# Attention scores of two heads side by side on 64 rows each, with queries and keys transposed before they are split

## The chip, the cores and the metric

The kernel runs on one core of a Trainium2 chip. The metric is the device time of one execution in microseconds (us); less is better. Engines: PE is TensorE (matmuls), PEld its weight loads, DVE VectorE, ACT ScalarE, POOL GpSimd, SP SyncE, which here only issues DMAs.

## The reference, cut to what matters

One inference step of a two-layer backbone with 640 tokens: 512 latent tokens, which are computed together with 128 prompt tokens. In every layer one input projection feeds three token mixers of head size 64; their outputs are gated, summed, projected, and followed by a squared-ReLU feed-forward. All is fp32.

```python
# A: differential attention, 4 pairs of heads, keys of 512 latent + 128 cached tokens
o1 = blocked_attention(q[:, :, :HA, None], k[:, :, :HA], v)[:, :, :, 0]
o2 = blocked_attention(q[:, :, HA:, None], k[:, :, HA:], v)[:, :, :, 0]
o = o1 - lam.astype(o1.dtype) * o2
# B: grouped-query attention, 8 heads of queries, 2 of keys, the same 640 keys
s = jnp.einsum('bqhgd,bkhd->bhgqk', qblk, k, preferred_element_type=jnp.float32) * scale
p = jax.nn.softmax(s, axis=-1).astype(v.dtype)
# C: neighbourhood attention, 8 heads: 256 keys around a tile of 128 queries, with a bias, and the 128 cached ones
p = jax.nn.softmax(jnp.concatenate([s_lat, s_ctx], axis=-1), axis=-1).astype(v.dtype)
```

The prompt's tokens attend to the 128 prompt keys alone.

## The kernel before, in words

**Precision.** The matmuls run on fp32r operands. Each fp32 operand is split in two parts: hi, a copy to fp32r (ACT), and lo, the rest (DVE, `value - hi`). A product with weights takes three matmuls: hi·hi, hi·lo, lo·hi. Transposes run on PE as well, through `tp` (line 246); every matmul goes through `mm` (line 243). As helpers record every operation, all ACT work stands under line 260, DVE's mostly under 265, with 278 for `stt`, and POOL's under 303 and 309.

**Issue order.** `Plan` (from line 56) records all instructions in program order and then writes down, with estimated durations, the order in which each engine issues them: each takes the first recorded of the instructions whose operands are there by the estimate (`schedule`, line 165). PSUM is followed bank by bank, in recorded order. `pl.bias` shifts an instruction's place in that order: the evacuation of a projection is moved forward (`EVAC`), the projection of mixers B and C back (`FILL`).

**Stages.** A layer has a mixer stage (`Phase1`) and then gates, branch and output projections and the feed-forward, which are products of 128 features by 640 tokens in pieces of 256 and 384 columns. The mixers go in 10 units of 384 columns of the input projection: 4 of A (two heads and one value of 128 each), 2 of B (four query heads, one key head), 4 of C (two heads). So the two layers have 8, 4 and 8 units. For each unit and each of 5 tiles of 128 tokens (order 0, 1, 4, 2, 3; tile 4 is the prompt), `project` (line 798) makes 24 matmuls of 384 columns into bank 0 or 1, and `evacuate` (line 806) takes the result apart: values, the norm in B, the rotary embedding in A and B, and then, from line 864, queries and keys. These are split into hi and lo while tokens still lie on partitions (two ACT and two DVE instructions), one of the two operands doubled, so that 128 columns hold hi and lo (or hi twice) of one head. Six fp32r transposes through bank 2 (`tz`) turn them, an ACT copy takes 512 columns out (scaled by 1/8) and a DVE copy 256.

**Scores.** Contraction rows 0 to 63 hold hi of a head's keys and rows 64 to 127 lo (for A and C), the queries are hi on both halves or lo on both. So two matmuls of 128 rows per head make all four products (`scores`, line 901; in B the roles are exchanged). `dense_row` (line 928) makes one head's scores of 128 queries by 640 keys in two banks of three (3, 4, 5), then the maximum (DVE), the exponential with its sum (ACT), and the row is scaled (POOL, in A the difference of the two heads). C takes 384 keys in one of the three banks.

**Values.** Probabilities are transposed in fp32, four blocks of 128 columns to a bank of `tb_` (banks 6 and 7), split while they leave PSUM (`split_T`, line 911), and multiplied with the values. In B and C a stationary tile holds hi and lo of the values, so the result's row halves are added (`fold`, line 1041). Outputs go to DRAM (`ospill`) and are read back by the next stage.

**Jobs.** A unit is 1 (A), 5 (B: four heads and the prompt) or 3 (C: two heads and the prompt) jobs of three stages: scores; transposes and values; A's norm. `step` (line 1185) records stage 3 of job i − 2, stage 1 of job i and stage 2 of job i − 1; the projections of the next unit are recorded after it.

## Time and profile before

| | |
|---|---|
| median of 3 runs | 2447.91 us (2447.16 to 2448.43) |
| span of the profiled execution, first to last instruction | 2446.9 us |
| another time of that execution | none is given; its span is the time that the rows are held against |
| instructions | 41996 |

The span is what the trace covers; the median is 1.0 us longer. A busy share counts the time in which at least one instruction of an engine is under way. Matmuls overlap in the array, so that the mean duration of one is longer than the distance from one to the next.

### The profile page before, as it was taken

To read this page: it belongs to the slowest core of one execution; us is meant where nothing else is said; L and a number is where in the kernel's file an instruction comes from. 1 tells how busy PE (TensorE), PEld (TensorE's weight loads), DVE (VectorE), ACT (ScalarE), POOL (GpSimd) and SP (SyncE) were. 2 spreads that over 40 slices of the span, in tenths; PEclk is the share of its full clock that TensorE was granted. 3 is DMA by queue.
4 is the path that set the end of the run, shared out by engine and by line. 5 is a ranking of instruction groups with operands and counts; after the bars stand their busy time and mean duration, and the time that the engine had idled before them with its cause. 6 is when DMAs were issued, how large, how long until landed. Compare 5 with 4: busy or idle time off the path is not lost. (4 is left out here: it accounts for less than half of the span.)

```text
span 2446.9 us, 41996 instructions
## 1 busy us (share of the span) xinstructions
PE 2376.5 (97%) x15796; PEld 2306.2 (94%) x15796; DVE 1601.8 (65%) x3615; ACT 1100.8 (45%) x2650; POOL 446.0 (18%) x527
## 2 busy tenths in 40 slices
PE   7898999999999999999999999999999999999998
PEld 5798999999999999999989988999999999999997
DVE  6878878789989994444477787765343674444445
ACT  4556677632333523222266567765223263223321
POOL 3536534200000000000034454321000000000000
PEclk8999999999999999999999999999999999999999
DMA  6211112466554552222231112225232222222221
GB/s 239 87 49 59 51 48 83 148 234 212 192 177 131 162 192 78 72 78 72 78 123 56 50 50 68 69 81 172 78 94 77 73 72 72 78 75 75 78 72 57
DMA packets 94960, 245.39 MB, mean 100 GB/s; under 512 B 11682, under 2 KB 23458, under 8 KB 93732
## 3 DMA queue, kind: packets, MB, share of 16 engines
q1 hardware_dynamic: 94756, 242.70, 30.5%
q8 instruction: 124, 2.03, 0.3%
q14 instruction: 80, 0.66, 0.1%
HBM read 225.62 MB, written 17.04 MB: 99 GB/s over the span
## 5 line engine op out<-in xcount | busy, mean ns | idle before, releaser
L243 PE MATMUL psm<-mr 128*128 128x384 f32 (+1 forms) x10656 | 1764.8, 319 | 17.6 <-ACT mr L260 8.6
L243 PEld LDWEIGHTS psm<-mr 128*128 128x128 f32 x10656 | 1631.2, 189 | 26.7 <-ACT mr L260 11.6
L260 ACT ACTIVATE mr<-mf 128x384 fp32r<-128x384 f32 (+2 forms) x928 | 445.3, 498 | 906.1 <-PE psm L243 868.4
L265 DVE TENSOR_TENSOR mr<-mf,mr 128x384 fp32r<-128x384 f32 (+3 forms) x796 | 419.3, 537 | 497.7 <-ACT mr L260 492.3
L309 POOL TENSOR_TENSOR mr<-mf,mr 128x384 fp32r<-128x384 f32 (+1 forms) x168 | 189.4, 1147 | 491.3 <-ACT mr L260 490.6
L243 PE MATMUL psm<-U,mr 128*128 128x256 f32 (+1 forms) x1788 | 277.6, 306 | 0.6 <-ACT mr L260 0.5
L243 PEld LDWEIGHTS psm<-U,mr 128*128 128x128 f32 x1788 | 264.4, 189 | 1.3 <-ACT mr L260 0.6
L309 POOL TENSOR_TENSOR mf<-mf 128x256 f32<-128x256 f32 (+3 forms) x93 | 89.9, 967 | 842.8 <-DVE mf L265 822.1
L303 POOL TENSOR_SCALAR mf<-mf 128x640 f32<-128x640 f32 (+3 forms) x236 | 144.3, 615 | 353.0 <-DVE mf L265 286.6
L292 DVE CUSTOM_DVE_ANT_0 psm<-mf,U1B 128x1024 f32<-128x1024 f32 x160 | 197.5, 1234 | 11.3 <-DMA mf<-wmod 9.9
L278 DVE SCALAR_TENSOR_TENSOR mf<-psm,mf 128x256 f32<-128x256 f32 (+2 forms) x484 | 171.3, 400 | 50.6 <-PE psm L243 42.2
L260 ACT ACTIVATE mf<-psm,mf 128x640 f32<-128x640 f32 (+3 forms) x256 | 162.5, 643 | 65.8 <-DVE mf L265 48.4
L260 ACT ACTIVATE mf<-mf 128x256 f32<-128x256 f32 (+5 forms) x305 | 140.4, 500 | 76.8 <-DVE mf L278 52.7
L265 DVE TENSOR_REDUCE mf<-psm 128x1 f32<-128x640 f32 (+2 forms) x212 | 148.2, 703 | 39.4 <-PE psm L243 33.8
L265 DVE TENSOR_TENSOR mr<-psm,mr 128x512 fp32r<-128x512 f32 (+2 forms) x252 | 140.9, 578 | 24.3 <-ACT mr L260 21.8
L260 ACT ACTIVATE mf<-psm 128x384 f32<-128x384 f32 (+7 forms) x266 | 104.1, 417 | 106.5 <-PE psm L243 102.5
L260 ACT ACTIVATE mr<-psm 128x512 fp32r<-128x512 f32 (+2 forms) x252 | 123.5, 513 | 53.2 <-PE psm L246 45.5
L246 PE MATMUL psm<-mf 128*128 128x128 f32 x752 | 119.6, 275 | 5.7 <-DVE mr L265 3.7
L265 DVE TENSOR_TENSOR mf<-psm,mf 128x128 f32<-128x128 f32 (+5 forms) x248 | 92.7, 390 | 46.2 <-ACT mf L260 24.3
L246 PEld LDWEIGHTS psm<-mf 128*128 128x128 f32 x752 | 89.8, 141 | 16.8 <-DVE mr L265 6.8
L246 PEld LDWEIGHTS psm<-mr 128*128 128x128 f32 x600 | 73.1, 141 | 33.5 <-DVE mr L265 20.1
L246 PE MATMUL psm<-mr 128*128 128x128 f32 x600 | 89.4, 242 | 12.4 <-DVE mr L265 9.5
(85 smaller groups left out, 1516.4 us busy)
## 6 DMA issues: line engine op xcount, KB each, us to landing
mf<-w SPq DMA_DIRECT2D x368, 384.0 KB, 3.0
mf<-wmod SPq DMA_DIRECT2D x84, 512.0 KB, 3.6
mf<-bias SPq DMA_DIRECT2D x8, 1024.0 KB, 5.2
U<-wmod SPq DMA_DIRECT2D x12, 512.0 KB, 5.9
mf<-x SPq DMA_DIRECT2D x16, 320.0 KB, 6.8
ospill<-mf SPq DMA_DIRECT2D x16, 256.0 KB, 2.4
newz<-mf SPq DMA_DIRECT2D x20, 192.0 KB, 1.9
U1A<-ospill SPq DMA_DIRECT2D x12, 320.0 KB, 2.9
```

Source lines behind the costliest of these rows:

```text
L243: self.add("PE", d, lambda R: self.nc.tensor.matmul(R(out), R(lhsT), R(rhs), start=start, stop=stop), [out], [lhsT, rhs])
L246: self.add("PE", 55 if in_.dtype == F32R else 108, lambda R: self.nc.tensor.transpose(R(out), R(in_), ident), [out], [in_, ident])
L260: self.add("ACT", d, lambda R: self.nc.scalar.activation(R(out), R(in_), func, **kw), outs, ins)
L265: self.add("DVE", d, lambda R: getattr(self.nc.vector, name)(R(out), *map(R, ins), *args, **kw), [out] + list(extra), list(ins) + [x for x ...
L278: self.add("DVE", d, lambda R: self.nc.vector.scalar_tensor_tensor(R(out), R(a), s, R(b), op0, op1), [out], [a, b] + ([s] if hasattr(s, "a ...
L292: self.add("DVE", d, lambda R: self.nc.vector.tensor_tensor_reduce(out=R(out), in0=R(a), in1=R(b), scale=1.0, scalar=0.0, op0=ALU.mult, op ...
L303: self.add("POOL", d, lambda R: self.nc.gpsimd.tensor_scalar(R(out), R(a), s1, s2, op0, op1), [out], [a] + [s for s in (s1, s2) if hasattr ...
L309: self.add("POOL", d, lambda R: self.nc.gpsimd.tensor_tensor(R(out), R(a), R(b), op), [out], [a, b])
```

## The change

- Queries and keys are no longer split before the transposes. Their fp32 values (in B after norm and rotary embedding, with the one key head copied beside itself by POOL; in C copied out of PSUM by ACT) are collected for tiles 0 and 1, for 4, and for 2 and 3 (`batch`), and then transposed in fp32, two heads of 64 features to a block: one block of queries (two in B) and one of keys per token tile. The transposes go through banks 6 and 7, and the split into hi and lo happens while the blocks leave PSUM.
- A head m has rows 64 m to 64 m + 63 of queries and keys. Its scores are three matmuls of 64 rows: hi·hi, hi·lo, lo·hi (lo·lo is dropped), recorded in turns for the two heads. Head 0 writes banks 2 and 4, head 1 banks 3 and 5 (`SC`); the prompt's scores go there too. `Plan.mm` counts half the time for a matmul of 64 rows.
- B's and C's jobs are now two heads by half of the latent tokens instead of one head by all. In C the value products of 4 × 512 columns per unit become 16 of 128 columns; those of 256 columns stay 16. Outputs of B and C are stored in halves of 256 tokens.
- Cached keys are no longer doubled in DRAM. The first unit's banks and the temporary places are rearranged, the feed-forward has 9 spare places instead of 10, comments are gone.

```diff
@@ Plan.mm
         if rhs.dtype == F32R:
             d = max(n, 256) / 2.4
+            if lhsT.ap[0][1] == 64:
+                d /= 2
@@ hybrid_plan
-    zb, tz, sb1, tb_ = Banks((0, 1)), psm[:, 2], Banks((3, 4, 5)), Banks((6, 7))
...
-            return (psm[:, 3:5], psm[:, 3:6:2], psm[:, 4:6])[(self.i - 1) % 3]
+    zb, tb_ = Banks((0, 1)), Banks((6, 7))
+
+    SC = [psm[:, 2 + m:6:2] for m in range(2)]
+    ROWSOF = (slice(0, 64), slice(64, 128))
+    PARTS = ((0, 0), (0, 1), (1, 0))
@@ Phase1
-            self.hl = r.ring(768, 2)
...
-            self.ck, self.cv = b.tile(256), b.tile(128)
+            self.ck, self.cv = b.tile(128), b.tile(128)
...
-            self.tmp = b.ring(320, 5)
+            self.src = b.ring(UW, 3)
+            self.tmp = b.ring(320, 4)
@@ Unit.cached
-            act(dst, ck, AF.Copy)
-            tt(dst[64:128], ck[64:128], f32(dst[64:128]), ALU.subtract)
+            self.split(self.kk[:, 0, k0:k0 + P], self.kk[:, 1, k0:k0 + P], ck)
@@ Unit.evacuate
+            elif self.k == "C":
+                src = p.src.get(nqk)
+                act(src, z[:, :nqk], AF.Copy)
...
-            self.split(t1[:, :, 0], t1[:, :, 1], s4[:, one])
-            self.split(t2[:, :, 0], t2[:, :, 1], s4[:, two].unsqueeze(2).to_broadcast([P, n2, 2, 64]))
-
-            tb = tz
-            for i in range(4):
-                tp(f32r(tb[:, i * P:(i + 1) * P]), hlt[:, i * P:(i + 1) * P], identr)
-            act(self.qall[:, :, c], tb.rearrange("p (f t) -> p f t", f=4), AF.Copy, scale=0.125)
-            for i in range(2):
-                tp(f32r(tb[:, i * P:(i + 1) * P]), hlt[:, (4 + i) * P:(5 + i) * P], identr)
...
+            ks = src[:, P:2 * P]
+            if self.k == "B":
+
+                ks = (p.src.get() if prompt else whole)[:, 2 * P:]
+                for h in range(prompt ^ 1, 2):
+                    pl.pts(ks[:, h * 64:(h + 1) * 64], src[:, 256:320], 1.0, 0.0, ALU.mult, ALU.add)
+            self.batch.append((t, src, ks))
+            if t in (1, 3, 4):
+                self.transposed()
+            pl.bias = 0
+
+        def transposed(self):
+
+            n, t0, nf = len(self.batch), self.batch[0][0], self.nf
+            m = n * P
+            c = slice(t0 * P, t0 * P + m)
+            qb = tb_.get()
+            kb, k0 = (tb_.get(), 0) if self.k == "B" else (qb, m)
+            for j, (_, src, ks) in enumerate(self.batch):
+                for f in range(nf):
+                    tp(qb[:, f * m + j * P:f * m + (j + 1) * P], src[:, f * P:(f + 1) * P], identf)
+                tp(kb[:, k0 + j * P:k0 + (j + 1) * P], ks, identf)
+            self.batch = []
+            qs = qb[:, :nf * m].rearrange("p (f t) -> p f t", f=nf)
+            act(self.q[:, :, 0, c], qs, AF.Copy, scale=0.125)
+            stt(self.q[:, :, 1, c], qs, 0.125, f32(self.q[:, :, 0, c]), ALU.mult, ALU.subtract)
...
+            for dst, d0, s0, s1 in pieces:
+                d = slice(d0, d0 + s1 - s0)
+                self.split(dst[:, 0, d], dst[:, 1, d], kb[:, k0 + s0:k0 + s1])
+
+
+        def scores(self, outs, f, c, keys):
+
+            for i, (x, y) in enumerate(PARTS):
+                for m in range(2):
+                    mm(outs[m], self.q[ROWSOF[m], f, x, c], keys(ROWSOF[m], y), i == 0, i == 2)
@@
-        def dense_row(self, h, c, sums):
...
+        def dense_rows(self, f, c, sums):
+
             for hf in range(2):
-                self.scores(sb[:, hf, :320], h, c, slice(hf * 320, (hf + 1) * 320))
-            nm = small.get()[:, :1]
-            pl.red(nm, sb[:, :, :320], AX.XY, ALU.max, negate=True)
+                kc = slice(hf * 320, (hf + 1) * 320)
+                self.scores([SC[m][:, hf, :320] for m in range(2)], f, c, lambda r, y: self.kk[r, y, kc])
+            rows = []
+            for m in range(2):
+                nm = small.get()[:, :1]
+                pl.red(nm, SC[m][:, :, :320], AX.XY, ALU.max, negate=True)
+                b, pt = self.p.pp.get()
+                act(pt.rearrange("p (f k) -> p f k", f=2), SC[m][:, :, :320], AF.Exp, bias=nm, accum=sums[m])
+                rows.append((b, pt))
+            return rows
@@ jobs
-                return [self.job_B(0, o), self.job_B_prompt()] + [self.job_B(m, o) for m in (1, 2, 3)]
-            o = {}
-            return [self.job_C(0, o), self.job_C_prompt(), self.job_C(1, o)]
+                return [self.job_B(0, 0), self.job_B_prompt(), self.job_B(0, 1), self.job_B(1, 0), self.job_B(1, 1)]
+            return [self.job_C(0), self.job_C_prompt(), self.job_C(1)]
@@ job_B
+            for qt in (2 * half, 2 * half + 1):
+                s = [small.get()[:, :1] for _ in range(2)]
+                r = self.dense_rows(f, slice(qt * P, (qt + 1) * P), s)
@@ job_C
+            for i, qt in enumerate((2 * half, 2 * half + 1)):
+                s3 = [SC[m][:, i, :384].rearrange("p (b k) -> p b k", b=3) for m in range(2)]
+                self.scores(s3, 0, slice(qt * P, (qt + 1) * P), lambda r, y: k5[r, y, blocks[qt]])
...
+            for m in range(2):
+                o0 = m * 256
+                for ch, c0 in ((4, 0), (1 if half == 0 else 3, 256)):
+                    todo += [(ob[:, o0:o0 + 256], self.v[:, ch, m], prs[m][s][:, c0:c0 + 256]) for s in range(2)]
+                for i in range(2):
+                    c0 = o0 + i * P
+                    todo += [(ob[:, c0:c0 + P], self.v[:, chunks[i], m], prs[2][s][:, c0:c0 + P]) for s in range(2)]
@@ layers
-    first_z = {t: psm[:, b, :UW] for t, b in zip(ORDER, (2, 0, 1, 3, 7))}
+    first_z = {t: psm[:, b, :UW] for t, b in zip(ORDER, (2, 0, 1, 3, 4))}
...
-                pl.dma(of, ospill[4 * b + i], keys_in=[("o", 4 * b + i, 0), ("o", 4 * b + i, NLAT)])
+                pl.dma(of, ospill[4 * b + i], keys_in=[("o", 4 * b + i, c) for c in (0, 256, NLAT)])
```

## Rows read from the trace of the kernel before

**Rows 1.** The page: span, and each engine's busy us, share and instructions.
```profile
span 2446.9 us, 41996 instructions
...
PE 2376.5 (97%) x15796; PEld 2306.2 (94%) x15796; DVE 1601.8 (65%) x3615; ACT 1100.8 (45%) x2650; POOL 446.0 (18%) x527
```

**Rows 2.** Busy time by stage: stretch, length, busy us (x instructions), granted clock, DMA share, GB/s.
```profile
core 0: us, PE busy (x) PEld busy (x) DVE busy (x) ACT busy (x) POOL busy (x), PEclk, DMA share, GB/s
87.00:490.00 403.00, 388.63 (x2540) 366.56 (x2540) 313.79 (x790) 267.74 (x711) 171.43 (x218) 0.99 0.22 73
490.00:1237.00 747.00, 745.20 (x5092) 743.85 (x5091) 528.54 (x1088) 251.81 (x538) 19.72 (x18) 1.00 0.43 138
1237.00:1672.00 435.00, 418.94 (x2693) 390.81 (x2693) 339.25 (x849) 293.26 (x777) 192.52 (x235) 1.00 0.23 75
1672.00:2447.00 775.00, 760.93 (x5188) 758.84 (x5186) 359.37 (x784) 250.80 (x540) 17.39 (x17) 0.99 0.26 81
```

**Rows 3.** PE's longest waits, 87 to 490 us, then 1237 to 1672: us, times, longest.
```profile
PE psm L246 <- DVE mr L265: 4.8, 8, 1.8
...
PE psm L246 <- DVE mr L265: 8.5, 14, 1.5
```

**Rows 4.** PE's groups by shape: operation, out<-in, shape, count, busy us, mean ns, idle before.
```profile
L243 PE MATMUL psm<-U 128*128 128x320 f32 x256 | 52.4, 318 | 0.6 <-DVE U L265 0.6
L243 PE MATMUL psm<-U 128*128 128x384 f32 x64 | 16.5, 348 | 0.0
L243 PE MATMUL psm<-U1B,U 128*128 128x128 f32 x48 | 7.0, 268 | 0.3 <-ACT mf L260 0.3
...
L243 PE MATMUL psm<-mr 128*128 128x384 f32 x6528 | 1706.5, 343 | 17.5 <-ACT mr L260 8.6 <-POOL mr L309 5.5 <-DVE mf L278 2.2
...
L243 PE MATMUL psm<-mr,U1B 128*128 128x512 f32 x92 | 23.9, 395 | 0.0
...
L246 PE MATMUL psm<-mr 128*128 128x128 f32 x600 | 89.4, 242 | 12.4 <-DVE mr L265 9.5 <-ACT mr L260 1.4 <-ACT U L260 0.3
L246 PE MATMUL psm<-mf 128*128 128x128 f32 x752 | 119.6, 275 | 5.7 <-DVE mr L265 3.7 <-DVE mf L265 0.8 <-DVE mf L278 0.3
```

**Rows 5.** PE's timeline in four short stretches of the mixers: start us, length us, what, count.
```profile
1501.04 0.74 PE L243 MATMUL psm<-U 128*128 128x320 f32 x4
...
265.80 1.03 PE L243 MATMUL psm<-mr 128*128 128x384 f32 x5
...
1499.66 1.55 PE L243 MATMUL psm<-mr,U1B 128*128 128x512 f32 x6
...
288.38 1.00 PE L243 MATMUL psm<-U1B,U 128*128 128x128 f32 x8
...
269.00 0.46 PE L246 MATMUL psm<-mr 128*128 128x128 f32 x4
...
332.30 0.60 PE L246 MATMUL psm<-mf 128*128 128x128 f32 x4
```

**Rows 6.** PE's timeline, 52.9 to 57.4 us, and the group of its first matmuls.
```profile
52.63 1.80 PE L243 MATMUL psm<-U,mf 128*2 128x128 f32 x15
54.37 2.88 PE L243 MATMUL psm<-mr 128*128 128x384 f32 x15
57.17 0.22 PE L246 MATMUL psm<-mf,U1A 2*128 2x2 f32 x1
...
L243 PE MATMUL psm<-U,mf 128*2 128x128 f32 x2 | 0.4, 272 | 0.0
```

**Rows 7.** Groups of DVE and ACT, 87 to 490 us, columns as in rows 4.
```profile
L265 DVE TENSOR_REDUCE mf<-psm 128x1 f32<-128x640 f32 x64 | 52.3, 818 | 15.0 <-PE psm L243 14.1 <-ACT mr L260 0.8
L265 DVE TENSOR_TENSOR mr<-mf,mr 128x256 fp32r<-128x256 f32 x34 | 18.5, 544 | 1.2 <-ACT mr L260 1.1
...
L260 ACT ACTIVATE mf<-psm,mf 128x640 f32<-128x640 f32 x64 | 50.8, 793 | 18.5 <-DVE mf L265 18.4
...
L260 ACT ACTIVATION_READ_ACCUMULATOR mf<-psm,mf 128x1 f32 x120 | 23.9, 199 | 0.0
```

More of the change, by code (lines that the diff above doesn't have):

```diff
@@ L863, in evacuate @@
                 src = rr
-            hlt = p.hl.get()
-            s4 = src[:, :nqk].rearrange("p (h d) -> p h d", h=nh)
+            ks = src[:, P:2 * P]
             if self.k == "B":
-                one, two = slice(0, 4), slice(4, 5)
-                t1, t2 = hlt[:, :512], hlt[:, 512:]
-            else:
-                one, two = slice(2, 4), slice(0, 2)
-                t1, t2 = hlt[:, 512:], hlt[:, :512]
-            n1, n2 = one.stop - one.start, two.stop - two.start
-            t1 = t1.rearrange("p (h s d) -> p h s d", h=n1, s=2)
@@ L939, in prompt_softmax @@
-        def prompt_softmax(self, n, scale=True):
-            sb = tb_.get()
-            for m in range(n):
-                self.scores(sb[:, m * P:(m + 1) * P], m, slice(NLAT, T), slice(0, P), True)
-            s3 = sb[:, :n * P].rearrange("p (m k) -> p m k", m=n)
-            nm, sums = small.get()[:, :n], small.get()[:, :n]
-            pl.red(nm, s3, AX.X, ALU.max, negate=True)
-            b, pt = self.p.pp.get()
-            for m in range(n):
-                act(pt[:, m * P:(m + 1) * P], s3[:, m], AF.Exp, bias=nm[:, m:m + 1], accum=sums[:, m:m + 1])
+                kc = slice(hf * 320, (hf + 1) * 320)
@@ new lines, in prompt_softmax @@
+        def prompt_softmax(self, scale=True):
+            nf = self.nf
+            for f in range(nf):
+                self.scores([SC[m][:, f, :P] for m in range(2)], f, slice(NLAT, T), lambda r, y: self.kp[r, y])
+            n = 2 * nf
+            nm, sums = small.get()[:, :n], small.get()[:, :n]
+            b, pt = self.p.pp.get()
+            for m in range(2):
+                pl.red(nm[:, m * nf:(m + 1) * nf], SC[m][:, :nf, :P], AX.X, ALU.max, negate=True)
+                for f in range(nf):
+                    i = m * nf + f
+                    act(pt[:, i * P:(i + 1) * P], SC[m][:, f, :P], AF.Exp, bias=nm[:, i:i + 1], accum=sums[:, i:i + 1])
@@ L1044, in fold, with folded, job_B @@
             tt(dst, ob[0:64], dst, ALU.add)
[L1046 to L1057 removed]
+        def folded(self, i, half, ob):
+            b, x = self.p.pp.get(256)
+            for m in range(2):
+                self.fold(x[ROWSOF[m]], ob[:, m * 256:(m + 1) * 256])
+            self.out(i, x, half * 256, half * 256 + 256)
+            self.p.pp.put(b)
+        def job_B(self, f, half):
             p = self.p
             rows = []
[L1060 to L1065 removed]
+            for qt in (2 * half, 2 * half + 1):
+                s = [small.get()[:, :1] for _ in range(2)]
+                r = self.dense_rows(f, slice(qt * P, (qt + 1) * P), s)
+                for m in range(2):
+                    self.scaled(r[m][1], s[m])
+                rows.append(r)
             yield
[L1067 removed]
+            prs = self.chunks_T([rows[i][m] for m in range(2) for i in range(2)])
             ob = tb_.get()
@@ new lines, in job_C @@
+            rows = []
+            for i, qt in enumerate((2 * half, 2 * half + 1)):
+                s3 = [SC[m][:, i, :384].rearrange("p (b k) -> p b k", b=3) for m in range(2)]
+                self.scores(s3, 0, slice(qt * P, (qt + 1) * P), lambda r, y: k5[r, y, blocks[qt]])
+                r = []
+                for m in range(2):
+                    tt(s3[m][:, window[qt]], s3[m][:, window[qt]], self.bias[:, m, qt], ALU.add)
+                    nm, s1 = small.get()[:, :1], small.get()[:, :1]
+                    pl.red(nm, SC[m][:, i, :384], AX.X, ALU.max, negate=True)
+                    b, pt = p.pp.get(384)
+                    act(pt, SC[m][:, i, :384], AF.Exp, bias=nm, accum=s1)
+                    self.scaled(pt, s1)
+                    r.append((b, pt))
+                rows.append(r)
@@ new lines, in job_C, with third @@
+            yield
+            def third(i, m, th):
+                return rows[i][m][1][:, th * P:(th + 1) * P]
+            both = ((0, 1), (2, 2)) if half == 0 else ((2, 1), (1, 0))
+            one, chunks = ((1, 0), (0, 2)) if half == 0 else ((0, 2), (2, 0))
+            prs = [self.blocks_T([third(i, m, th[i]) for th in both for i in range(2)]) for m in range(2)]
+            prs.append(self.blocks_T([third(i, m, one[i]) for m in range(2) for i in range(2)]))
+            for r in rows:
+                for b, _ in r:
+                    p.pp.put(b)
@@ L1293, in hybrid_plan @@
         rm = rmem()
-        us_ = Pieces([u0[:, i * T:(i + 1) * T] for i in range(11)] + [u1[:, i * T:(i + 1) * T] for i in range(6)] + [rm.tile(T) for _ in range(10)])
+        us_ = Pieces([u0[:, i * T:(i + 1) * T] for i in range(11)] + [u1[:, i * T:(i + 1) * T] for i in range(6)] + [rm.tile(T) for _ in range(9)])
         if not last:
```

174 lines of the change are left out of this document (48 added, 126 removed).

## The prediction

> **What bounds the kernel now.** I read the page first, then the busy time by stage, then what TensorE (PE) waits for, then the groups of its instructions by shape. The page shows PE busy for 97% of the span, VectorE (DVE) 65%, ScalarE (ACT) 45%, GpSimd (POOL) 18% [rows 1]. The table by stage splits this: two mixer stages (87 to 490 us and 1237 to 1672 us, 838 us together) in which PE is busy 388.63 of 403 and 418.94 of 435 us and DVE 78%, and two stages of plain products in which PE is never free (745.20 of 747); PE's granted clock is 0.99 to 1.00, the 2.4 GHz level, in all four [rows 2], and I count on no change of it. The change touches the mixers alone. There PE's idle time is small (14.4 and 16.1 us), and a good two fifths of it is one wait: the transposes of line 246 for DVE's half of the split, 4.8 and 8.5 us [rows 3]. So PE sets the time of these stages, nearly instruction by instruction, and the sum is made of PE's instructions.
>
> A matmul's own duration holds its way through the array, so a price is taken from a piece of the timeline as (length − one duration)/(count − 1), with the durations of the groups [rows 4, 5]: scores of 320 columns (0.74 − 0.318)/3 = 0.141 us; matmuls of 384 columns (1.03 − 0.343)/4 = 0.172; a value product of 512 columns (1.55 − 0.395)/5 = 0.231; 128 columns, the prompt's scores, (1.00 − 0.268)/7 = 0.105; a transpose of fp32r (0.46 − 0.242)/3 = 0.073; one of fp32 (0.60 − 0.275)/3 = 0.108.
>
> **The scores.** Before, the two layers issue 512 scores of 320 columns, 128 of 384 and 96 of the prompt [rows 4] (of each kind one of two like rows stands there): 72.2 + 22.0 + 10.1 = 104.3 us. After, a tile of 128 queries takes three passes for each of two heads: mixer A 8 units × 4 tiles × 2 halves × 6 = 384, B 4 × 8 × 2 × 6 = 384, C 8 × 4 × 6 = 192 of 384 columns, and the prompt 8 × 6 + 8 × 6 + 4 × 12 = 144. No row shows a matmul on 64 rows beside another. Ends: each alone at the price of a full one, 108.3 + 33.0 + 15.1 = 156.4 us (+52); or two in the time of one, since two times 64 rows fill the 128 that one matmul fills today, 78.2 us (−26). Write f for the share that runs as a pair: +52 − 78f.
>
> The change's order decides f. A pair needs its two matmuls next to each other in PE's order, and the plan takes the first recorded instruction that is ready. Head 0 now owns banks 2 and 4, head 1 banks 3 and 5, and there is no second set: the next tile's scores of a head wait for its exponential. The maxima of the two heads go one after the other on DVE (0.818 us each), the exponentials on ACT (0.793 and 0.199 to read the sum) [rows 7]. So head 1's banks come free about 1.0 us behind head 0's, longer than head 0's six matmuls take even at a full price (6 × 0.141 = 0.85), and these go out as a run of their own, six on the same rows. The heads start together only where their banks were idle: the first tile of an A unit (1 of 4) and of a B unit (1 of 8), and two of four in C, whose tiles alternate between two banks a head: 8 + 4 + 16 = 28 of 96. With some more that find PE held by earlier value products, I take f = 0.4: +21 us, ends +52 and −26.
>
> A rule beside this: in the Trainium skill, "TensorE: Matmul & The Clock Gate", Part 3 (The mechanism), matmuls on different row groups run at once, starting about 4 ns apart, and matmuls start in program order. That is the lower end for a pair, and it gives a lone run nothing; no run here shows either.
>
> **Leaving the full array.** The trace has a change of the array's use, in the start: matmuls with 2 columns, then full ones, then a transpose on 2 rows [rows 6]. The fifteen of 2 columns last 1.80 us, so by (1.80 − 0.272)/14 they come 0.109 apart and the last starts at 54.16; the first full one follows at 54.37, 0.21 later, 0.10 late. The fifteen full ones take 2.80 us to the next start where 15 × 0.172 is 2.58. So a way in and a way out together cost about 0.10 + 0.22, say 0.3 us. The 64-row scores would make such stays between full matmuls: 64 tile rows in A and B, 32 in C, 20 prompts = 116 if the heads go together, twice that if each goes alone, 116 × (2 − f) = 186 at f = 0.4. At 0.3 us: 56 us. Ends: nothing (64 rows might not count as another shape), and 232 × 0.3 = 70. I take the row, as the transpose on 2 rows, too, takes only part of the array's rows. Nothing hides it: PE is the engine that is full.
>
> **Transposes.** Out: 20 units × 5 tiles × 6 = 600 of fp32r [rows 4], 600 × 0.073 = 44 us. In: A and C 16 × 5 × 2, B 4 × 5 × 3, 220 of fp32, 24 us. −20 us. The wait for DVE's split ahead of them (13.3 us [rows 3]) goes too, but the new ones wait for POOL's sum of the rotary embedding or ACT's copy, in 60 batches instead of 200; I take half, −7, ends −13 and +10. Behind a waiting transpose stand projections and value products on PE, and the scores of the unit need it.
>
> **DVE and ACT.** Of each of 100 token tiles three DVE and three ACT instructions go (two splits and the way out of PSUM); each of 60 batches gets two (C three for the tokens): 136 on each engine, and ACT 32 copies more in C. At some 0.45 us (a split of 256 columns takes 0.544 [rows 7]) DVE loses 164 × 0.45 = 74 us of 653 in the two stages, and ACT about 60. This is beside PE's work, and worth only what PE waits for them: −10 us, ends 0 and −20. POOL gets 24 small copies in B, hidden under PE; B's last score waits for one at most.
>
> **Value products in C.** Out 4 per unit of 512 columns, 32 in all (7.4 us); in 16 of 128 columns per unit, 128 × 0.105 = 13.4 us: +6. Those of 256 columns stay 128. In A and B their number stays.
>
> **Banks 6 and 7.** Queries and keys now pass through the banks of the value products, in recorded order, where bank 2 was their own: the value stage of the unit before stands behind the transposes of the next unit's last tile. Work that hides it: the projections of the unit after. I cost it at nothing; without that cover it is about 1.6 us (four reads of a bank at 0.4) at 19 unit borders, +30.
>
> **At nothing, together:** the other banks of the first unit, one place fewer in the feed-forward, smaller cached keys, and 16 more stores on SP's queue (outputs in halves), behind which only later loads stand; the first product that reads them comes after eight gate products. If that cover were gone, one landing of some us.
>
> **Sum.** +21 + 56 − 20 − 7 − 10 + 6 = +46 us on the span of 2446.9; the page names no other time for that execution, and the median of the runs, 2447.91, is 1.0 above it: 2494 us. About 0.2% (5 us) is what a measurement of this kernel can tell from no change.
>
> **Rivals.** (1) The heads stay in step. Place: the order of the score matmuls (line 243) at each tile. If all pair, −26 + 35 − 31 = −22, 2426 us, faster. With the other terms as above the change of the time is 91 − 113f, so it decides from f = 0.81 on. For it: three chains share DVE and ACT, and PE, being full, may come late enough to find both heads ready. Against: the 1.0 us between the heads [rows 7]. Chance 0.20. (2) A stay on 64 rows costs nothing: 52 − 31 − 31 = −10 at f = 0.4, 2438 us; against it, a way in and a way out that both cost [rows 6]. Chance 0.12; with (1) on top −57, 2391. (3) Side by side doesn't happen, the change doesn't do what it says: +52 + 70 − 31 = +91, 2539 us. Chance 0.15. The forecast keeps 0.53.
>
> Another rule speaks against the change: in the same page, LDWEIGHTS, loading 128 columns takes 128/1.2 = 107 ns however many rows there are. The trace agrees for the full array, 0.105 us in the prompt's run [rows 5]; were two such loads to follow each other, a pair would take 0.21 instead of 0.14, which by an estimate makes the sum +62, 2510 us.
>
> **How the numbers follow.** The likeliest case gives 2494; its own range, with f from 0.2 to 0.6 (±23) and the ends of the small terms, is 2460 to 2525. The range reaches past (1) and just to (3): 2415 to 2539. Faster: (1) and (2) less 0.03 that falls within 5 us, 0.29; same 0.07, those 0.03 and 0.04 of the forecast's lower edge; slower 0.64, the rest of the forecast and (3).
>
> **What would show it.** Right: runs of 64-row scores of one head six at a time, alternating at about 1 us; 320-column scores of one head 0.14 apart; gaps of 0.1 us at their borders; 220 fp32 transposes in place of 600; DVE some 35 us lighter in each mixer stage; both mixer stages longer by about 20 us and the others unchanged. Wrong: scores in runs of twelve with starts in twos, or no gap where they begin and end; then the mixers get shorter.

## The result and the profile after

The changed kernel takes 2570.02 us (median of 4 runs, 2568.17 to 2577.94) where the kernel before, beside it on the same chip, takes 2447.53: ratio 1.051 [1.049, 1.052]. The direction was forecast, the size was not: +46 us forecast, +122 measured. The profiled execution is the longest of the four (2577.94 us); its span is 2576.2 us, 129.3 above that of before, and the rows below are held against this one. In the changed kernel `mm` is line 245, `tp` 248, ACT's work 262, DVE's 267.

The page, against [rows 1], and the busy time by stage, against [rows 2]. The stretches are moved so that the two stages of plain products keep their lengths.

```profile
span 2576.2 us, 42060 instructions
...
PE 2490.2 (97%) x15880; PEld 2339.8 (91%) x15880; DVE 1533.2 (60%) x3487; ACT 1058.7 (41%) x2550; POOL 439.4 (17%) x551
```
```profile
core 0: us, PE busy (x) PEld busy (x) DVE busy (x) ACT busy (x) POOL busy (x), PEclk, DMA share, GB/s
87.00:556.50 469.50, 448.47 (x2555) 383.69 (x2554) 276.40 (x722) 245.33 (x658) 168.72 (x229) 0.93 0.19 62
556.50:1303.50 747.00, 744.74 (x5090) 743.37 (x5089) 529.40 (x1085) 250.43 (x536) 18.22 (x16) 1.00 0.42 137
1303.50:1801.00 497.50, 473.40 (x2764) 407.34 (x2763) 306.94 (x790) 275.79 (x730) 189.51 (x248) 0.97 0.21 67
1801.00:2576.00 775.00, 761.01 (x5181) 758.74 (x5179) 359.19 (x786) 249.95 (x541) 17.22 (x17) 0.99 0.25 80
```

The whole loss is in the mixers: 469.5 us against 403, and 497.5 against 435. The clock column is the surprise: 0.93 and 0.97. By the trace's records of the clock, 61.4 and 34.1 us of the two stages, 95.6 in all, are at the lower level, 1.2 GHz; before it was 10.2.

PE's waits over the whole span, the ones that answer to [rows 3] last:

```profile
PE psm L245 <- DVE mf L267: 16.2, 28, 2.5
PE psm L245 <- ACT mf L262: 11.4, 19, 1.0
...
PE psm L248 <- DVE mr L267: 5.2, 4, 1.6
```

But for some 4 us of the first, which lie outside the mixers, the first two are matmuls, nearly all of scores, that wait until the maximum (DVE) or the exponential (ACT) has read their bank. The kernel before has these two lines as well, and none of its 4.2 us is a score:

```profile
PE psm L243 <- DVE mf L265: 4.2, 4, 2.6
...
PE psm L243 <- ACT mf L260: 1.2, 3, 0.5
```

The third line is no longer the wait for the split: it is transposes of probabilities that wait until DVE has read their bank. Of the 13.3 us that stood there before, 9.5 were the split and 3.7 this wait [rows 4].

PE's groups by shape, against [rows 4]; then one group each of DVE and ACT in the first mixer stage, against [rows 7], hardly changed:

```profile
L248 PE MATMUL psm<-mf 128*128 128x128 f32 x972 | 165.9, 283 | 14.3 <-DVE mr L267 5.2 <-DVE mf L267 3.1 <-ACT mf L262 1.7
...
L245 PE MATMUL psm<-U 64*128 64x320 f32 x384 | 71.3, 339 | 8.7 <-ACT mf L262 4.8 <-DVE mf L267 3.3
L245 PE MATMUL psm<-U1A 64*128 64x320 f32 x384 | 68.9, 336 | 12.8 <-DVE mf L267 7.8 <-ACT mf L262 4.0
...
L245 PE MATMUL psm<-U 64*128 64x384 f32 x96 | 18.5, 378 | 0.0
...
L245 PE MATMUL psm<-U1B,U 64*128 64x128 f32 x72 | 15.7, 348 | 0.0
L245 PE MATMUL psm<-U1A 64*128 64x384 f32 x96 | 15.4, 367 | 0.5 <-ACT U1A L262 0.5
...
L245 PE MATMUL psm<-U1B,U1A 64*128 64x128 f32 x72 | 13.9, 308 | 2.7 <-ACT mf L262 2.6
```
```profile
L267 DVE TENSOR_REDUCE mf<-psm 128x1 f32<-128x640 f32 x64 | 51.9, 822 | 50.4 <-PE psm L245 38.8 <-ACT mf L262 11.4
...
L262 ACT ACTIVATE mf<-psm,mf 128x640 f32<-128x640 f32 x64 | 50.7, 793 | 41.9 <-DVE mf L267 29.6 <-PE psm L245 7.0 <-issue 3.9
```

All 1104 score matmuls and 220 more fp32 transposes (972 for 752) are there. The scores keep PE busy for 203.7 us (the six groups), against 151.8 before [rows 4, with the like rows counted twice]. PE's timeline, the first mixer stage, 104.7 to 113.6 us:

```profile
104.67 0.86 PE L245 MATMUL psm<-mr 128*128 128x384 f32 x4
105.46 1.14 PE L245 MATMUL psm<-U 64*128 64x320 f32 x6
106.53 2.01 PE L245 MATMUL psm<-mr 128*128 128x384 f32 x10
108.49 0.71 PE L245 MATMUL psm<-U 64*128 64x320 f32 x3
109.65 0.55 PE L245 MATMUL psm<-U 64*128 64x320 f32 x2 [0.44 <-ACT mf L262]
110.13 0.44 PE L248 MATMUL psm<-mf 128*128 128x128 f32 x2
110.50 0.41 PE L245 MATMUL psm<-U 64*128 64x320 f32 x1
110.84 0.79 PE L245 MATMUL psm<-mr 128*128 128x384 f32 x3
111.90 1.71 PE L245 MATMUL psm<-U 64*128 64x320 f32 x6 [0.27 <-DVE mf L267]
```

Read from top to bottom this is the loss in small. Six matmuls of one head go out alone and hold PE from 105.46 to 106.53, 1.07 us. The next six come in pieces of three, two and one, with a stop for an exponential and a way out and in between. Then a stop for a maximum, and the six after it last 1.71 us, since the clock fell at 112.2. Call a run of 64-row matmuls with no other shape in between a stay. Counted over the whole timeline, the 1104 lie in 211 stays (87 of six, 50 of three), and 194 of 552 pairs start together, within 0.04 us.

PE's time can also be summed from the start of each instruction to the start of the next, with waits of over 0.15 us and half of the time at half clock taken out. By this sum the 129 us are: half clock 42.9, waits 14.6, value products 4.5, transposes −13.2, and the scores with all matmuls around them 80.2.

### The profile page after: what moved, and what is told of

It reads as the page before. It is cut to its first block, busy times and chain, and to the rows that moved or that the text cites. A ratio compares the mean times of both kernels' runs of the same rounds, so it can differ in the third digit from the quotient of the medians.

```text
span 2576.2 us, 42060 instructions
## 1 busy us (share of the span) xinstructions
PE 2490.2 (97%) x15880; PEld 2339.8 (91%) x15880; DVE 1533.2 (60%) x3487; ACT 1058.7 (41%) x2550; POOL 439.4 (17%) x551
## 5 line engine op out<-in xcount | busy, mean ns | idle before, releaser
L245 PEld LDWEIGHTS psm<-mr 128*128 128x128 f32 x10528 | 1623.0, 190 | 43.8 <-issue 18.6
L262 ACT ACTIVATE mr<-mf 128x384 fp32r<-128x384 f32 (+2 forms) x792 | 405.3, 522 | 892.8 <-PE psm L245 863.7
L267 DVE TENSOR_TENSOR mr<-mf,mr 128x384 fp32r<-128x384 f32 (+2 forms) x656 | 357.2, 552 | 488.2 <-ACT mr L262 482.9
L305 POOL TENSOR_SCALAR mf<-mf 128x640 f32<-128x640 f32 (+4 forms) x260 | 144.9, 563 | 447.8 <-DVE mf L267 405.6
L267 DVE TENSOR_REDUCE mf<-psm 128x1 f32<-128x640 f32 (+3 forms) x232 | 149.4, 657 | 113.4 <-PE psm L245 92.0
L262 ACT ACTIVATE mf<-psm 128x256 f32<-128x256 f32 (+6 forms) x330 | 122.0, 390 | 171.5 <-PE psm L245 155.9
L248 PE MATMUL psm<-mf 128*128 128x128 f32 x972 | 165.9, 283 | 14.3 <-DVE mr L267 5.2
L248 PEld LDWEIGHTS psm<-mf 128*128 128x128 f32 x972 | 116.8, 143 | 45.7 <-issue 12.1
L245 PE MATMUL psm<-U1A,mr 128*128 128x256 f32 (+1 forms) x608 | 109.9, 309 | 0.0
L245 PE MATMUL psm<-U 64*128 64x320 f32 (+1 forms) x480 | 89.8, 347 | 8.7 <-ACT mf L262 4.8
```

The lines of the kernel that those rows point to most:

```text
L245: self.add("PE", d, lambda R: self.nc.tensor.matmul(R(out), R(lhsT), R(rhs), start=start, stop=stop), [out], [lhsT, rhs])
L248: self.add("PE", 55 if in_.dtype == F32R else 108, lambda R: self.nc.tensor.transpose(R(out), R(in_), ident), [out], [in_, ident])
L262: self.add("ACT", d, lambda R: self.nc.scalar.activation(R(out), R(in_), func, **kw), outs, ins)
L267: self.add("DVE", d, lambda R: getattr(self.nc.vector, name)(R(out), *map(R, ins), *args, **kw), [out] + list(extra), list(ins) + [x for x ...
L305: self.add("POOL", d, lambda R: self.nc.gpsimd.tensor_scalar(R(out), R(a), s1, s2, op0, op1), [out], [a] + [s for s in (s1, s2) if hasattr ...
```

## The experiments

Theory A: the heads are out of step, and all of the loss follows from that (matmuls without partner, more ways into and out of rows of 64, stops, half clock). The rivals: another part of the change, the plan's price, a plan that is too tight, the rows of 64 as such.

**All rows** (the price in the plan stays half):

```diff
-                    mm(outs[m], self.q[ROWSOF[m], f, x, c], keys(ROWSOF[m], y), i == 0, i == 2)
+                    mm(outs[m], self.q[:, f, x, c], keys(slice(0, P), y), i == 0, i == 2, score=True)
```

> The changed kernel with its six score matmuls per pair of heads left in their order, but each on all 128 rows: both heads' rows enter, so the scores are the sum of the two heads' and the outputs are not the reference's. No change of the array's use, no pairs. Theory A, the 64-row shape is the loss (runs of one head, 0.3 us per way in and out, and a granted clock that falls in them): 63 us of ways in and out and some 43 us of half clock go, 26 us of pairing are lost, about 2490 us, half clock in the mixers under 20 us. Theory B, the new order and banks 6 and 7 make PE stop and the clock falls for that: about 2530 us or more, half clock still over 70 us.

2514.79 us, ratio 1.028 [1.026, 1.030], 3 us of half clock in the mixers. Between the two forecasts: time as B has it nearly, clock as A. The waits for maximum and exponential are 19.4 and 17.3 us, longer than in the changed kernel. By the prediction's prices 1104 full scores for 736 cost +52, the transposes −20, the values +6, these waits +31 (36.7 − 5.4): +69, and the span is +66.8. PE's order is that of the changed kernel but for two instructions, and the stops are there; the clock did not follow them. The waits, then the changed kernel around the fall at 112.2, then this one in the same stretches:

```profile
PE psm L245 <- DVE mf L267: 19.4, 32, 2.6
PE psm L245 <- ACT mf L262: 17.3, 38, 1.0
```

```profile
108.00:112.20 4.20, 3.49 (x17) 2.11 (x16) 1.43 (x5) 2.24 (x8) 0.00 (x0) 1.00 0.13 47
112.20:125.90 13.70, 13.70 (x44) 12.26 (x43) 4.92 (x18) 5.24 (x15) 4.12 (x6) 0.50 0.02 7
```
```profile
108.00:112.20 4.20, 3.29 (x20) 2.70 (x20) 1.50 (x5) 1.70 (x7) 0.79 (x1) 1.00 0.13 47
112.20:125.90 13.70, 13.66 (x87) 13.10 (x86) 9.46 (x24) 8.10 (x22) 9.60 (x12) 1.00 0.20 63
```

**Four passes**: as above, without the third pass, so PE's work is that of before, less the transposes' 20 us.

```diff
-                d /= 2
+                d *= 0.75
...
-            for i, (x, y) in enumerate(PARTS):
+            for i, (x, y) in enumerate(PARTS[:2]):
```

> As the run on all rows, with the third pass left out too, so four matmuls of 128 rows per pair of heads as in the kernel before (outputs not the reference's). It leaves the rest of the change: fp32 transposes through banks 6 and 7, splits out of PSUM, jobs by halves. Theory A: about 2430 us, 15 to 20 under the kernel before, since 220 transposes take the place of 600. Theory B: 2470 us or more.

2484.45 us, 1.016 [1.014, 1.017]: A missed, B as forecast. Waits for exponential and maximum are 29.0 and 19.1 us, half clock 20.5. The sum −20 + 6 + 43 (waits) + 5 (half clock) = +34 against a span of +33.7. So the stops do not need 64 rows; whether they come with the heads out of step, the eighth experiment asks.

**In step**: the plan's book-keeping counts banks 2 and 3, and 4 and 5, as one during the mixers; nothing else is changed.

```diff
-            return [("P", b) for b in {x // 512 for x in last}]
+            banks = {x // 512 for x in last}
+            if self.pairs:
+                banks |= {b - b % 2 for b in banks if 2 <= b < 6}
+            return [("P", b) for b in banks]
```

> The changed kernel with the two banks of a pair of heads counted as one in the plan, so that both heads' scores come free together and stand next to each other. Theory A with pairs at the price of one: some 116 runs instead of 211, 52 us of score time and 28 us of ways in and out go, and part of the half clock: 2470 us, give or take 20. [...] Theory B: the heads now wait for each other, 2560 or more.

2446.96 us, 1.000 [0.999, 1.001], 3 us under A's range: the whole loss is gone, and nothing is won on the kernel before. 133 stays instead of 211, 534 of 552 pairs together, half clock 13.7 us. Its timeline (`mm` is line 249) and its groups:

```profile
102.67 1.15 PE L249 MATMUL psm<-U 64*128 64x320 f32 x12
103.75 4.43 PE L249 MATMUL psm<-mr 128*128 128x384 f32 x24
108.11 1.25 PE L249 MATMUL psm<-U 64*128 64x320 f32 x12
```
```profile
L249 PE MATMUL psm<-U1A 64*128 64x320 f32 x384 | 41.1, 335 | 2.1 <-ACT mf L266 2.1
L249 PE MATMUL psm<-U 64*128 64x320 f32 x384 | 40.2, 328 | 0.2
```

Twelve matmuls hold PE from 102.67 to 103.75, 1.08 us, where six took 1.07; the 768 scores of 320 columns take 81.3 us instead of 140.2, and their waits shrink from 21.5 us to 2.3.

**Scores alone**: no part of the reference; stretches of the same matmuls without any wait, written as loops of their own.

```python
        full(300); same(300); full(150); lone(300); full(150); pair(300); full(150)
        for _ in range(40):
            lone(6); full(6)
```

> Only stretches of matmuls, outputs not computed: 300 of 128 rows and 320 columns, 300 of 64 rows on the same rows, 300 pairs of 64 rows, between them 150 of 384 columns, then 40 times six and six of each sort with 384 columns. Theory A: lone ones 0.141 apart at most as dense as full ones and the granted clock at half within that stretch, so 0.27 apart; pairs 0.141 a pair at the full clock; alternating with full ones, 0.3 us more per six and six. Theory B: the granted clock stays at full in all stretches.

The timeline: full rows, one half of the rows, both halves in turns, then six and six in turns.

```profile
62.20 44.15 PE L36 MATMUL ps<-one 128*128 128x320 f32 x300
106.19 26.19 PE L36 MATMUL ps<-two 128*128 128x384 f32 x150
132.31 44.26 PE L36 MATMUL ps<-one 64*128 64x320 f32 x300
...
202.71 44.27 PE L36 MATMUL ps<-one 64*128 64x320 f32 x600
...
273.11 1.14 PE L36 MATMUL ps<-one 64*128 64x320 f32 x6
274.18 1.32 PE L36 MATMUL ps<-two 128*128 128x384 f32 x6
275.43 1.14 PE L36 MATMUL ps<-one 64*128 64x320 f32 x6
```

300 alone take 44.26 us, as long as on full rows, and 600 in pairs 44.27: a pair is two in the time of one, 0.148 us. Six and six come round in 2.32 us (275.43 − 273.11) where 6 × 0.148 + 6 × 0.175 is 1.94: a way in and out costs 0.38 here. Six pairs and six full ones come round in the same 2.32 us further on, and six and six of 320 and 384 columns, both on full rows, in 1.94. The granted clock is 1.00 in all of these stretches, as B has it, so rows of 64 without stops don't lower it; single matmuls, then pairs:

```profile
132.00:176.00 44.00, 44.00 (x301) 43.75 (x300) 0.00 (x0) 0.00 (x0) 1.00 0.00 1
202.00:246.00 44.00, 44.00 (x595) 43.75 (x595) 0.00 (x0) 0.00 (x0) 1.00 0.01 2
```

The Trainium skill, "TensorE: Matmul & The Clock Gate", Part 3 (The mechanism), lets matmuls on different row groups run at once, and this trace agrees: the two of a pair start 3 ns apart. From the Trainium skill's section "LDWEIGHTS (loading the stationary operand)" on the same page, columns/1.2 ns for a load, the prediction had its estimate of 0.21 us for a pair whose loads follow each other; the measured 0.148 shows that the loads for different rows don't add up.

**Plan price**: the changed kernel without the half price.

```diff
-            if lhsT.ap[0][1] == 64:
-                d /= 2
```

> The changed kernel with one edit: the plan prices a score matmul of 64 rows at a full pass (133 ns) instead of half of one. The order that comes out has 212 runs of such matmuls between others, against 211 in the changed kernel and 133 where the two banks count as one. Theory A (the heads fall out of step because the plan hands out the two score banks one by one, as each is read): no better, 2555 to 2585 us, some 80 to 110 us of half clock in the mixers. Theory B (the half price drives them apart): below 2500 us and below 30 us of half clock.

2597.08 us, 1.061 [1.060, 1.063], 109 us of half clock: A, and 12 us past its range. The half price isn't what drives the heads apart; without it fewer pairs start together, 165, and the time is longer.

**Banks 6 and 7**: the kernel before with its transposes there, and the first unit's banks as in the change.

```diff
-            tb = tz
+            tb = tb_.get()
...
+            tb = tb_.get()
             for i in range(2):
...
-    first_z = {t: psm[:, b, :UW] for t, b in zip(ORDER, (2, 0, 1, 3, 7))}
+    first_z = {t: psm[:, b, :UW] for t, b in zip(ORDER, (2, 0, 1, 3, 4))}
```

> The kernel before with one part of the change: the transposes of queries and keys go through banks 6 and 7, which they share with the transposes of the probabilities, instead of through a bank of their own. Theory A (the sharing costs nothing, as predicted: what waits for bank 2 now waits for bank 6 or 7): 2440 to 2452 us. Theory B (the upper end of the prediction's bound): 2465 us or more, with the wait moved to the transposes of the probabilities.

2545.83 us, 1.041 [1.039, 1.043]: far past B. PE's longest waits, 100 to 500 us, and then, in the columns of [rows 2], the stretch ahead of one fall of the clock and the fall:

```profile
PE psm L246 <- DVE mr L265: 8.9, 12, 1.4
PE psm L246 <- DVE mf L265: 5.2, 5, 1.8
PE psm L243 <- ACT mf L260: 3.3, 5, 1.5
```
```profile
163.00:167.60 4.60, 2.91 (x23) 2.27 (x21) 2.44 (x9) 3.01 (x11) 0.00 (x0) 1.00 0.03 7
167.60:174.40 6.80, 6.07 (x30) 5.36 (x31) 6.40 (x18) 4.12 (x11) 2.84 (x5) 0.50 0.00 0
```

Over the whole span PE's waits grow by 52 us (111.6 against 59.8), and 65 us of the mixers run at half clock, worth 27 more than before ((64.9 − 10.2)/2). Of the 95.6 us of span that leaves 17, and by the sum from start to start 16 of these are in the transposes themselves, 137.7 us against 121.4. As B has it, the transposes of probabilities wait longer, 32.7 us against 5.7, but those of queries and keys do too, 21.7 against 12.4. Two things follow: half clock comes without any row of 64; and a part of the change that I costed at nothing costs a lot in the order of before.

**Half the transposes**: the kernel before with the new fp32 transposes of two heads at once, each head's parts then written above each other by instructions of 64 rows; the core of the edit for A and C:

```diff
+            tp(tz[:, :P], src[:, :P], identf)
+            tp(tz[:, P:2 * P], src[:, P:2 * P], identf)
+            for m in range(2):
+                for r in range(2):
+                    act(self.q[rows[r], m, 0, c], qb[rows[m]], AF.Copy, scale=0.125)
+                    stt(self.q[rows[r], m, 1, c], qb[rows[m]], 0.125, f32(self.q[rows[r], m, 0, c]), ALU.mult, ALU.subtract)
```

> The kernel before with another part of the change: queries and keys are transposed unsplit in fp32, two heads in one transpose, and split into high and low part while leaving the bank; the scores stay two passes of 128 rows per head, so each head's parts are written above each other by instructions of 64 rows (12 to 14 per tile on ScalarE and VectorE in place of 6). 180 transposes in fp32 take the place of 600 in fp32r, by the prediction's prices about 14 us less of TensorE. Theory A (the mixers are bounded by TensorE, the added narrow instructions lie beside it): 2430 to 2441 us. Theory B (the keys come later and TensorE waits for them): 2447 us or more, with longer waits of score matmuls for the parts.

2528.46 us, 1.034 [1.032, 1.035]: B. PE waits 16.5 and 16.3 us where before it waited 4.2 and 1.2 (the line of the maximum, of which only some 5 are scores here, and that of the exponential), 13.7 in the transposes until VectorE has emptied their bank into the keys, and 8.6 in other matmuls, 6.8 of it scores, for the low part of the keys; 34 us of half clock. Saved transposes are worth nothing if what follows them comes later. Here scores wait for exponentials although the heads still take turns in three banks, so two heads on one set of banks are not the only way to such stops.

**In step, four passes**: the second experiment with the third one's edit.

```diff
+            if self.pairs:
+                banks |= {b - b % 2 for b in banks if 2 <= b < 6}
```

> The second experiment (each of two passes per head on all 128 rows, third pass left out, so the output is not the reference's; 2484 us) with the two banks of a pair counted as one in the plan, as in the third. TensorE's work is then that of the kernel before, less some 20 us of transposes, with no row of 64. Theory A (all that the second experiment lost is the heads out of step, which makes matmuls wait for the maximum and the exponential of a bank): 2420 to 2440 us, waits for those two below 15 us together. Theory B (the rest of the change, the shared banks 6 and 7 among it, costs 20 us or more): 2460 us or more.

2435.53 us, 0.996 [0.994, 0.997]: A. Waits for exponential and maximum are 6.5 and 4.9 us, 11 together where the second experiment had 48: there the stops came from the heads out of step. The span is 13.8 us shorter than before, and −20 + 6 is −14: with the heads in step little is left for banks 6 and 7, or for any other part, to cost. It isn't nothing: all of PE's waits are 73 us here and 60 before, and by the sum from start to start the transposes are worth −24. Against the third experiment this one, whose scores are not the reference's, is some 11 us faster: with the heads in step, three passes in pairs on 64 rows cost more than two on full rows.

**Stops alone**: no part of the reference; groups of matmuls with a stop behind each.

```python
        for kinds in (("lone",), ("whole",), ("pair",), ("lone", "full"), ("whole", "full"), ("pair", "full")):
            for _ in range(40):
                for kind in kinds:
                    group(kind, 6)
                stop()      # ScalarE reads the bank of the group
            full(150)
```

> Nothing of the reference is computed; matmuls with stops in between, to see what the granted clock falls on. Six stretches of 40 groups: six lone matmuls of 64 rows; six of 128 rows; six pairs of 64 rows; and the same three with six of 128x384 behind them. After each group ScalarE reads the bank that the next group writes, so TensorE stops. Between the stretches 150 matmuls of 128x384 without a stop. Theory A (the falls of the changed kernel come from the rows of 64 together with stops): half clock in the stretches with lone 64-row matmuls, full clock in the two with 128 rows and nothing else. Theory B (the stops alone bring them, as the sixth experiment with 65 us of half clock and no row of 64 suggests): half clock in the stretches of 128 rows with stops as well, in step with their idle share.

Inconclusive. The matmuls without a stop were moved into the stops, so PE was busy 20.00 of 20 us nearly everywhere. One stretch came out with stops, of pairs on 64 rows (some of their records are missing):

```profile
220.00:280.00 60.00, 43.75 (x368) 34.78 (x368) 14.99 (x35) 0.00 (x0) 1.00 0.00 1
```
```profile
228.82 1.25 PE L36 MATMUL ps<-one 64*128 64x320 f32 x10 [0.47 <-ACT out L58]
230.54 1.25 PE L36 MATMUL ps<-one 64*128 64x320 f32 x10 [0.48 <-ACT out L58]
```

A stop of 0.47 us in every 1.73, for 60 us, and the clock stays at 1.00. So between pairs, stops of this length, evenly spread, don't lower it; single matmuls and full rows with such stops were not measured.

**Longer stays**: the third experiment, and the plan takes a 64-row matmul that is ready ahead of all else if the last one was of 64 rows.

```diff
+                if e == "PE" and inside:
+                    x = min((v for v in avail[e] if v[1] in self.half), default=x)
```

> The third experiment with one more edit to the plan: after a 64-row matmul it takes another one that is ready before anything else, and it prices each change of shape at 150 ns. The order has 121 runs of 64-row matmuls instead of 133, 63 of them of twelve instead of 53. Theory A (each way in and out costs 0.30 us, all else equal): 12 x 0.30 = 4 us less than the third experiment, 2440 to 2446 us. Rival B (keeping them together holds up other work that the engines wait for): above 2450 us.

2447.1 us, 1.0005 [0.9996, 1.0014]: between the two, no change. The scores, from a first start to the next start of a full matmul, take 113.7 us against 112.0 of the third experiment, so twelve stays fewer won nothing. They are not the only difference: 483 pairs start together here, 534 there.

**Slack**: the changed kernel with one number.

```diff
-SLACK = 0
+SLACK = 400
```

> The changed kernel with one number of its plan changed: results of other engines count as 400 ns later for TensorE than their prices say. The heads stay out of step (216 runs of 64-row matmuls against 211), but TensorE should find fewer results missing. Theory A (the loss is the lost pairing and the ways in and out; waits and half clock come on top): waits for maximum and exponential below 10 us, half clock below 40 us, and 2490 to 2530 us, since some 80 more ways in and out than in step (25 us) and some 40 us of matmuls without a partner stay. Theory C (the plan was only too tight; heads out of step cost nothing by themselves): below 2465 us.

2574.41 us, 1.053 [1.051, 1.055]: both missed. 109 us of half clock, waits for maximum and exponential 19.8 us. That the plan is too tight is not the cause, and moving work about in an order that stays out of step doesn't help.

**In step with slack**: the tenth experiment with the same line.

```diff
-SLACK = 0
+SLACK = 400
```

> The tenth experiment with the same 400 ns. 117 runs of 64-row matmuls, 67 of twelve. Theory A (in step, what is left to win is the waits of the mixers, some 20 us, of which the plan now avoids a part): 2425 to 2442 us, faster than both kernels. Rival B (work put off is only waited for elsewhere): 2445 us or more.

2459.79 us, 1.006 [1.004, 1.007]: B; half clock 34 us, with the heads in step (530 pairs).

**A pair as one item**: the changed kernel's banks, but the plan sees the two matmuls of a pair as one instruction.

```diff
-                for m in range(2):
-                    mm(outs[m], self.q[ROWSOF[m], f, x, c], keys(ROWSOF[m], y), i == 0, i == 2)
+                pl.mms([(outs[m], self.q[ROWSOF[m], f, x, c], keys(ROWSOF[m], y), i == 0, i == 2) for m in range(2)], 150)
```

> The changed kernel with the two matmuls of a pair given to the plan as one item of 150 ns; the banks are counted one by one as in the changed kernel. 140 runs of 64-row matmuls, every one with its partner behind it. Theory A (partners side by side and few ways in and out are what counts): 2442 to 2455 us, half clock below 25 us. Theory D (the later release of the banks in the third experiment's plan was what helped, by leaving TensorE something to do while a bank is read): above 2480 us with waits for maximum and exponential above 20 us.

2448.61 us, 1.0007 [0.9998, 1.0016], half clock 10 us: A. 525 pairs start together. A second way to put the heads in step gives the same time, so it is the step and not the third experiment's way of getting there.

**A block as one item**: the same with all six matmuls of a score block.

```diff
-                pl.mms([(outs[m], self.q[ROWSOF[m], f, x, c], keys(ROWSOF[m], y), i == 0, i == 2) for m in range(2)], 150)
+            pl.mms([(outs[m], self.q[ROWSOF[m], f, x, c], keys(ROWSOF[m], y), i == 0, i == 2)
+                    for i, (x, y) in enumerate(PARTS) for m in range(2)], 750)
```

> As the experiment before it, with the six matmuls of a score block as one item of 750 ns. 110 runs, 74 of them of twelve, the fewest of all. Theory A (0.30 us for each way in and out): 23 runs less than the third experiment, up to 7 us less: 2436 to 2447 us. Rival B (what the tenth experiment showed: fewer ways in are paid for in waits): 2447 us or more.

2449.88 us, 1.0014 [1.0006, 1.0023]: B. 110, 121, 133 and 140 stays all give 2447 to 2450 us, where 30 stays should be worth 9. Here the transposes wait more (7.4 us for `mf`, 4.1 in the experiment before). By the sum from start to start, scores and the matmuls around them take 5 us less than in the third experiment, and waits, transposes, value products and half clock 7 us more: what fewer ways win is spent there.

## Why the prediction was wrong in size

The sum again, each term by its rows. The first three have the measured counts at the forecast's prices:

| term | forecast | from the runs |
|---|---|---|
| score matmuls, 52 − 78f | f = 0.4: +21 | f = 194/552 = 0.35: +25 |
| ways in and out, 0.30 us each | 186: +56 | 211: +63 |
| transposes | −20 | −20 (the count is as forecast) |
| waits of the transposes | −7 | −4 (12.4 + 5.7 [rows 4] to 14.3) |
| PE's waits for maximum and exponential ("DVE and ACT") | −10 | +22 (5.4 to 27.6) |
| value products in C | +6 | +6 (4.5 from start to start) |
| granted clock | 0 | +43 ((95.6 − 10.2)/2) |
| sum | +46 | +135 (span +129.3) |

By the sum from start to start, scores and ways are 80 together, not 88, and the transposes −13: the prices are good to some 8 us.

**Right:** f and its reason, the way the single set of banks pulls the heads apart (the share beyond 28 of 96 was a guess, so that 0.35 is so near 0.4 is partly luck, and one stay starts some 3 us after the last in the median, not 1); that a way in and out costs, though 0.30 is low: in the timeline the first of the six at 105.46 is 0.09 us late, the six take 0.18 more, and the second full matmul behind them comes 0.28 us after the first instead of 0.175, 0.38 in all, as in the scores alone; DVE lighter by 37 and 32 us in the stages; plain products unchanged. Rival (3) fell: side by side happens. Rival (2) fell: the ways cost. Two readings were wrong beside the sum: 3.7 of the 13.3 us were no wait for the split, and against the load rule stands a price of the prediction's own, a transpose of fp32r in 0.073 us [rows 5], each with a load of 128 columns.

**Wrong, first step:** "DVE and ACT … worth only what PE waits for them: −10 us". The prediction saw that "there is no second set: the next tile's scores of a head wait for its exponential", and used it for f alone. It is also a stop of PE, 27.6 us in the two lines of waits where 5.4 stood: DVE and ACT have less to do, but what they do stands now directly in PE's way. Before, three banks took turns between heads.

**Wrong, second step, and the larger:** "I count on no change" of the clock. Stops of 0.27 and 0.44 us, as in the timeline, are small in the table of waits, but 13 of the 15 falls of the clock in the mixers follow a stretch with scores on 64 rows and stops of 0.24 to 1.38 us, the longest lasts 13.7 us, and PE is full, so half of that time is lost. (The two others, 3.4 us each, follow stops of 1.59 and 0.99 us without a row of 64, and the first experiment has one like them.) That is the +43 of the table. The Trainium skill, in "TensorE: Matmul & The Clock Gate", under "A second HAM failure mode: psum-queue depth-cycling", tells of short idles between groups of matmuls, as PSUM banks turn over, that take the clock back and forth; this trace agrees, with the falls at 112.2, 279.5 and 1525.3 us, behind stops of 0.44 and 0.27, 0.79 and 0.79 us. But the first experiment has the same order and longer stops, on full rows, and only one fall; why the clock falls in the one and not in the other stays open.

**Rival (1)** was right as a mechanism and wrong in price. In step, f = 534/552 = 0.97: −24 + 133 × 0.30 − 20 + 6 = +2, without any relief of waits, and the span is −2.0. Its 2426 us counted a relief of 17 us of waits, of which little came: in place of the transposes' waits for the split (9.5 us of the group in [rows 4]) those for an emptied bank grew from 3.7 to 8.7 us. The sum from start to start agrees: scores and the matmuls around them +2, transposes −16, waits +6, value products +7, half clock −1. Pairs that change the shape 133 times only win back what the ways in and out cost.

**Banks 6 and 7 at nothing** holds in the changed kernel with the heads in step (the eighth experiment), but its bound of +30 would not have held the kernel before, where the move alone costs 98 us.

## What to carry to other kernels

Two matmuls that share the array run together only if they are handed out together (194 of 552 pairs here, 534 in step): give the planner the pair as one item, or one name for its banks, and count the sets of banks before counting on pairs. On a full PE a wait has two prices, its own length and the half clock that may follow; where a change makes waits short and frequent, put both in the range. A stay on 64 rows costs 0.38 us of PE. Twelve matmuls as six pairs save two times 0.148 us on eight of full rows, less than that, so here pairs would pay only in longer stays.

## What the runs showed of the hardware

- A way into and out of rows of 64 costs 0.38 us, at the stay at 105.46 us of the changed kernel as where six and six alternate, with single matmuls or pairs; between 320 and 384 columns on full rows a change costs nothing (1.94 us a round). A pair costs as much as one, 0.148 us, its weight loads among it.
- Half clock came after stops in a kernel with full rows only (65 us, PE busy 2.91 of the 4.6 us ahead of a fall), and after a busier stretch with single 64-row matmuls (3.49 of 4.20 us), but not with full rows in the same place (3.29 of 4.20), not with dense 64-row matmuls, and not with pairs and a stop in every 1.73 us. At 112.2 us of the changed kernel it stayed down for 13.7 us in which PE was busy throughout. Part of the busy time of a stretch with changes of shape is a way in or out, in which for 0.1 us no matmul starts; whether that is what separates these cases is not shown.
